# Weight blocks split in one cast and one subtraction of 128x1024 in a hybrid decoder step

## The chip, the cores and the metric

The kernel runs on one core of one Trainium2 chip. The metric is the device time of one execution in microseconds (us). Before the change the median of three runs is 1835.99 us (1828.75 to 1836.97).

## The reference, cut to what matters

The reference is one layer of a decoder over 256 prompt tokens and 8 sample tokens (264 columns in the kernel). Nearly all of its work is a chain of large matrix products:

```python
z = h @ p['w_in'][l]                       # 2048 x 15376
(z_uv, hq, hf, hi, hg, gq, gk, gv, gr, glr, z_gate) = jnp.split(z, offsets, axis=-1)
...                                        # three token mixers: gMLP, HGRN2, GLA
merged = merged + gates[:, :, n_b] * (branches[n_b] @ p['w_branch'][l, n_b])
out = merged @ p['w_out'][l]
x = x + gt1 * rmsnorm(out, p['g_post_mix'][l])
...
y2 = jnp.square(jax.nn.relu(h2 @ p['w_mlp_up'][l])) @ p['w_mlp_down'][l]
x = x + gt2 * rmsnorm(y2, p['g_post_mlp'][l])
```

The two recurrent mixers also read and write a state for each of the 8 samples. All data are fp32.

## The kernel before, in words

**The arithmetic.** A product in fp32 is made of three products in the format fp32r. Each operand is split in a high part (a cast) and a low part (the operand less its high part); `granule` (L649) adds high x high (L659), high x low (L660) and low x high (L661) in PSUM. The activations are split once. The weights are split as they arrive, by the helper `split` (L108): a cast on ScalarE (ACT, L109) and a subtraction on VectorE (DVE, L110, recorded as L106, the line of `sub`). The subtraction reads what the cast wrote.

**Weight blocks.** The class `Stream` (L590) walks through a list of 578 weight blocks, made by `plan` in the order in which TensorE (PE) uses them. A block holds 1024 numbers in each of 128 partitions: four rows of 128x256 in most cases, two rows of 128x512 in the first twenty blocks and in the first MLP product. PE uses a block in 24 matmuls of 264 columns (L659 to L661).

**Stages of a block.** `load` (L596) fetches the block by one DMA, issued from SyncE's queue (SP, L616), into one of four `raw` buffers. Blocks 20 to 71 are fetched in pairs, so that each of two tiles holds a half of two blocks (L598 to L612). `split_half` (L619) splits one half of a block, 128x512, into a tile `whi` and a tile `wlo`; `split` (L626) does so for both halves. The pool `splp` has six buffers for each of the two kinds, which is three blocks. `ahead` (L631) is called before and after the matmuls of a block: it splits two blocks beyond the one in hand and loads up to five beyond it. So, once the matmuls of block i have been issued, block i+3 is split; its two halves go into the buffers that the two halves of block i leave.

**Use.** `granule` takes a block's two pairs of tiles and goes through its rows: rows of the first half first. Where a block has two accumulators (the first twenty blocks and the first MLP product), it goes through all rows for the first accumulator, then through all rows for the second. The accumulators have two buffers (`pmm`), and are emptied by ACT (L825) or DVE (`add`, recorded as L103).

**Order.** PE, SP and GpSimd (POOL) keep the order in which the program is written. In most stages ACT and DVE get theirs from a scheduler that places each instruction when the program is built, and both engines work strictly in that order. Two kinds of other work stand among the splits: evictions of PSUM, and work of the mixers that `background` (L699) deals out between blocks. Among the latter are the sample states (`samples_r`): POOL issues DMAs for a state `st` and for a row of values `vbc`, and ACT (L1103) and DVE (L1105) then update the state. Those two instructions wait for their DMAs, and what is queued behind them on ACT and DVE waits too.

## Time and profile before

| what | value |
| --- | --- |
| median of three runs | 1835.99 us (1828.75 to 1836.97) |
| the profiled execution, its own time | 1832.18 us |
| its span in the trace | 1830.4 us |
| mean TensorE clock granted | 0.997 of full speed |
| busy share: PE, DVE, ACT, POOL | 98%, 65%, 55%, 7% |
| moved by DMA | 442.05 MB, 242 GB/s over the span |

How to read it. Busy time is the time in which at least one instruction of an engine was running; a matmul's end is modelled, so a busy PE need not be at its peak. A row of a group of instructions gives the source line, the engine and operation, what is written and read, the tile's size and the number of instructions; behind the bar stand the total busy time, the mean of one in ns, and the engine's idle time ahead of them with what ended it. A row of the waits reads "who waited <- for whom: us in total, times, longest". In the timeline a row has start, duration, engine, line and operation; in brackets stands the idle time before it and what ended it. "PEld" is the weight load of a matmul.

### The profile page before, as it was taken

What the parts mean: (1) busy time and instruction counts of PE and PEld (TensorE: products, weight loads), DVE (VectorE), ACT (ScalarE), POOL (GpSimd) and SP (SyncE); (2) the same over time, 40 slices, a digit from 0 to 9 for tenths busy, and PEclk for the clock granted to TensorE, in tenths of its full rate; (3) what the DMA queues carried; (4) which work ended last, traced back from release to release, by engine and by line L of the source; (5) the groups of instructions that cost most, each with busy time, mean ns of one, the idle gap of its engine ahead of it and who ended that gap; (6) DMA issues with size and microseconds to landing.
All of it is one profiled execution on the core that took longest, in us unless ns stands there. A gap on an engine that the chain in (4) does not pass through costs nothing.

```text
span 1830.4 us, 42186 instructions
## 1 busy us (share of the span) xinstructions
PE 1788.7 (98%) x17012; PEld 1696.5 (93%) x17012; DVE 1181.8 (65%) x2092; ACT 1000.3 (55%) x1818; POOL 131.3 (7%) x210
## 2 busy tenths in 40 slices
PE   6999999999999999999999999999999999999998
PEld 4889999989988999989999989999999999999997
DVE  4566677787576696566555667555666666666666
ACT  5544364666755765654445666555554545454544
POOL 4221000111111101210000000000000000000000
PEclk9999999999999999999999999999999999999999
DMA  9999697788787788897987964777666666666663
GB/s 326 354 343 304 195 304 231 215 266 276 239 287 233 229 270 278 274 323 250 308 254 265 327 180 146 246 256 227 191 197 194 197 194 196 195 195 196 196 196 106
DMA packets 330179, 442.05 MB, mean 242 GB/s; under 512 B 14946, under 2 KB 276944, under 8 KB 329984
## 3 DMA queue, kind: packets, MB, share of 16 engines
q1 hardware_dynamic: 311728, 380.26, 65.0%
q0 software_dynamic: 17184, 57.85, 9.1%
q8 instruction: 133, 2.18, 0.5%
q10 hardware_dynamic: 1072, 1.25, 0.2%
q14 instruction: 62, 0.51, 0.1%
HBM read 427.60 MB, written 11.70 MB: 240 GB/s over the span
## 4 chain that ended last, share of the span: by engine, by line
PE 88%; DMA 2%; DVE 2%; issue 1%; ACT 1%; POOL 0%; DVEq 0%; ACTq 0%; POOLq 0%
PE mm L659 27%; PE mm L661 26%; PE mm L660 26%; PE ada L376 3%; DMA vbc<-vs_d 1%; PE ada L308 1%; DVE wlo L106 1%; PE sm L851 1%; PE sm L1208 1%; PE sm L679 1%; PE sm L686 1%; DMA raw<-in_w_in_dram 0%; DVE b L106 0%; PE sm L1578 0%; ACT whi L109 0%
## 5 line engine op out<-in xcount | busy, mean ns | idle before, releaser
L659 PE MATMUL mm<-b,whi 128*128 128x264 f32 x4624 | 1292.4, 279 | 12.3 <-issue 5.1
L661 PE MATMUL mm<-b,wlo 128*128 128x264 f32 x4624 | 1279.7, 277 | 5.1 <-DVE wlo L106 4.5
L660 PE MATMUL mm<-b,whi 128*128 128x264 f32 x4624 | 1278.8, 277 | 0.8 <-DVE b L106 0.7
L106 DVE TENSOR_TENSOR wlo<-raw,whi 128x512 fp32r<-128x512 f32 x1136 | 774.4, 689 | 489.1 <-ACT whi L109 475.0
L109 ACT CAST whi<-raw 128x512 fp32r<-128x512 f32 x1136 | 691.8, 616 | 644.5 <-DVE wlo L106 331.7
L659 PEld LDWEIGHTS mm<-b,whi 128*128 128x128 f32 x4624 | 875.8, 189 | 53.0 <-issue 28.0
L661 PEld LDWEIGHTS mm<-b,wlo 128*128 128x128 f32 x4624 | 876.2, 189 | 7.3 <-DVE wlo L106 7.2
L660 PEld LDWEIGHTS mm<-b,whi 128*128 128x128 f32 x4624 | 876.2, 189 | 4.4 <-issue 3.0
L103 DVE TENSOR_TENSOR b<-b,mm 128x528 f32<-128x528 f32 (+1 forms) x137 | 95.7, 699 | 24.5 <-PE mm L661 13.0
L1105 DVE SCALAR_TENSOR_TENSOR st<-vbc,b,st 128x128 f32<-128x128 f32 (+1 forms) x96 | 34.2, 390 | 55.2 <-DMA vbc<-vs_d 50.4
L1103 ACT ACTIVATE st<-st,fs 128x128 f32<-128x128 f32 (+1 forms) x96 | 37.1, 430 | 50.5 <-DMA st<-in_state_hgrn_dram 26.9
L488 POOL DMA_DIRECT2D b<-in_w_ada_dram x64 | 46.2, 724 | 126.0 <-PE ada L308 94.4
L376 PE MATMUL ada<-araw,cT 128*32 128x512 f32 x296 | 39.8, 601 | 0.0
L308 PE MATMUL ada<-b,cT 128*32 128x256 f32 (+1 forms) x640 | 35.1, 356 | 2.8 <-DMA b<-in_w_ada_dram 2.6
L100 DVE TENSOR_TENSOR b<-b,b 128x512 f32<-128x512 f32 (+1 forms) x47 | 33.9, 741 | 1.3 <-ACT b L1221 1.0
L1106 POOL DMA_DIRECT2D out_dram<-st x32 | 23.6, 736 | 130.5 <-DVE st L1105 130.5
L308 PEld LDWEIGHTS ada<-b,cT 128*32 128x32 f32 x640 | 17.8, 113 | 14.9 <-DMA b<-in_w_ada_dram 6.2
L376 PE MATMUL ada<-b,cT 128*32 128x512 f32 x216 | 26.2, 594 | 0.0
L106 DVE TENSOR_TENSOR b<-gt,b 128x528 fp32r<-128x528 f32 x32 | 22.7, 710 | 3.2
L106 DVE TENSOR_TENSOR b<-b 128x1024 f32<-128x1024 f32 (+1 forms) x24 | 24.3, 1017 | 0.0
L1632 ACT ACTIVATE b<-vt 128x528 fp32r<-128x528 f32 x32 | 23.0, 719 | 1.0
L106 DVE TENSOR_TENSOR b<-b,b 128x1056 fp32r<-128x1056 f32 (+3 forms) x21 | 20.8, 991 | 4.0 <-ACT b L109 3.8
(344 smaller groups left out, 854.0 us busy)
## 6 DMA issues: line engine op xcount, KB each, us to landing
raw<-in_w_in_dram SPq DMA_DIRECT2D x231, 512.0 KB, 4.8
raw<-in_w_mlp_up_dram SPq DMA_DIRECT2D x128, 512.0 KB, 3.9
raw<-in_w_mlp_down_dram SPq DMA_DIRECT2D x128, 512.0 KB, 3.7
araw<-in_w_ada_dram SPq DMA_DIRECT2D x74, 512.0 KB, 5.7
b<-in_w_ada_dram SPq DMA_DIRECT2D x54, 512.0 KB, 6.6
b<-in_w_ada_dram POOLq DMA_DIRECT2D x48, 512.0 KB, 8.9
raw<-in_w_branch_dram SPq DMA_DIRECT2D x48, 512.0 KB, 4.5
raw<-in_w_out_dram SPq DMA_DIRECT2D x32, 512.0 KB, 5.3
```

What stands on the lines that cost most here:

```text
L100: V.tensor_tensor(o, a, b, op=ALU.mult)
L103: V.tensor_tensor(o, a, b, op=ALU.add)
L106: V.tensor_tensor(o, a, b, op=ALU.subtract)
L109: S.copy(hi, src)
L308: T.matmul(acc[32 * j:32 * j + 32, 0:n], cT[:, k, :], w[:, n * j:n * j + n], start=k == 0, stop=k == KT - 1)
L376: T.matmul(self.acc[32 * j:32 * j + 32, :], cT[:, k, :], ws[j // 2][:, j % 2 * 512:j % 2 * 512 + 512], start=k == 0, stop=k == KT - 1)
L488: queue.dma_start(w[:, i], w1[k * P:(k + 1) * P, :, self.k0 * P:(self.k0 + self.n) * P])
L659: T.matmul(o, a, xh(k + j), start=first and j == 0, stop=False)
L660: T.matmul(o, a, xl(k + j), start=False, stop=False)
L661: T.matmul(o, b, xh(k + j), start=False, stop=last and j == n - 1)
L1103: S.activation(st[:, i, :], st[:, i, :], AF.Copy, scale=fs[:, h0 + i, b:b + 1])
L1105: V.scalar_tensor_tensor(st[:, i, :], v[:, i, :], k[:, h0 + i, NP + b:NP + b + 1], st[:, i, :], ALU.mult, ALU.add)
```

## The change

Each block that arrives in one tile is split by one cast and one subtraction of 128x1024. The `whi` and `wlo` tiles hold a whole block in every case, and there are three buffers of each kind instead of six of half the size. The first block (fetched by two DMAs) and the paired blocks 20 to 71 are still cast and subtracted in halves, which go into slices of the whole tile. In `granule` the matmuls read slices of one pair of tiles; their order is the same.

```diff
-SPLIT_BUFS = 6
+SPLIT_BUFS = 3
...
-            self.raw[i] = [t[:, 0:n // 2, :], t[:, n // 2:n, :]]
-
-        def split_half(self, i):
+            self.raw[i] = [t[:, 0:n // 2, :], t[:, n // 2:n, :]] if i == 0 else [t]
+
+        def split_next(self, i):
             n, width = self.items[i][2], self.items[i][4]
-            hi = splp.tile([P, n // 2, width], F32R, tag="whi", name=nm("whi"))
-            lo = splp.tile([P, n // 2, width], F32R, tag="wlo", name=nm("wlo"))
-            split(self.raw[i].pop(0), hi, lo)
-            self.parts.setdefault(i, []).append((hi, lo))
+            if i not in self.parts:
+                hi = splp.tile([P, n, width], F32R, tag="whi", name=nm("whi"))
+                lo = splp.tile([P, n, width], F32R, tag="wlo", name=nm("wlo"))
+                self.parts[i], self.done[i] = (hi, lo), 0
+            src = self.raw[i].pop(0)
+            js = slice(self.done[i], self.done[i] + src.shape[1])
+            self.done[i] = js.stop
+            split(src, *(v[:, js, :] for v in self.parts[i]))
...
-        h = n // 2
...
-                    a, b = (p[:, j % h, m * P:(m + 1) * P] for p in parts[j // h])
+                    a, b = (p[:, j, m * P:(m + 1) * P] for p in parts)
```

More of the change, by code (lines that the diff above doesn't have):

```diff
@@ L593, in __init__ @@
         def __init__(self, items):
-            self.items, self.raw, self.parts, self.at = items, {}, {}, 0
+            self.items, self.raw, self.parts, self.done, self.at = items, {}, {}, {}, 0
         def load(self, i):
@@ L616, in load @@
                 nc.sync.dma_start(t[:, a:b, :], w[(k + a) * P:(k + b) * P, c0:c0 + width].rearrange("(k p) c -> p k c", p=P))
-            self.raw[i] = [t[:, 0:n // 2, :], t[:, n // 2:n, :]]
-        def split_half(self, i):
+            self.raw[i] = [t[:, 0:n // 2, :], t[:, n // 2:n, :]] if i == 0 else [t]
+        def split_next(self, i):
             n, width = self.items[i][2], self.items[i][4]
-            hi = splp.tile([P, n // 2, width], F32R, tag="whi", name=nm("whi"))
-            lo = splp.tile([P, n // 2, width], F32R, tag="wlo", name=nm("wlo"))
-            split(self.raw[i].pop(0), hi, lo)
-            self.parts.setdefault(i, []).append((hi, lo))
+            if i not in self.parts:
[6 more added lines that the diff above has]
+            split(src, *(v[:, js, :] for v in self.parts[i]))
         def split(self, i):
             while self.raw[i]:
-                self.split_half(i)
+                self.split_next(i)
             del self.raw[i]
@@ L797, in hybrid_step_kernel @@
     rows = first.rows()
-    stream[0].split_half(0)
+    stream[0].split_next(0)
     next(rows)
@@ L802, in hybrid_step_kernel @@
     run(rows)
-    stream[0].split_half(0)
+    stream[0].split_next(0)
     for k, ps in zip((4, 6), early):
```

## The prediction

> **What bounds the kernel now.** I read the page's totals first, then the forty slices, then who waits for whom.

> ```profile
> span 1830.4 us, 42186 instructions
> PE 1788.7 (98%) x17012; PEld 1696.5 (93%) x17012; DVE 1181.8 (65%) x2092; ACT 1000.3 (55%) x1818; POOL 131.3 (7%) x210
> ...
> L106 DVE TENSOR_TENSOR wlo<-raw,whi 128x512 fp32r<-128x512 f32 x1136 | 774.4, 689 | 489.1 <-ACT whi L109 475.0
> L109 ACT CAST whi<-raw 128x512 fp32r<-128x512 f32 x1136 | 691.8, 616 | 644.5 <-DVE wlo L106 331.7
> ```

> PE is busy for 98% of the span: 41.7 us of idle are all that any change on ACT and DVE can win back. The instructions that the change merges are the largest users of DVE and ACT, but neither engine is full. The slices (PE, PEld, DVE, ACT, POOL busy, then clock, DMA share, GB/s) show three kinds of stage:

> ```profile
> 45.80:91.50 45.70, 42.88 (x494) 38.74 (x496) 25.20 (x43) 23.45 (x42) 12.25 (x17) 1.00 0.96 354
> 549.10:594.90 45.80, 42.94 (x500) 40.66 (x501) 30.51 (x56) 26.54 (x54) 6.64 (x10) 0.96 0.74 233
> 777.90:823.70 45.80, 43.11 (x383) 40.40 (x382) 28.07 (x59) 23.28 (x46) 6.71 (x10) 1.00 0.94 323
> 1372.80:1418.60 45.80, 45.80 (x409) 45.80 (x409) 28.89 (x43) 22.12 (x36) 0.00 (x0) 1.00 0.65 194
> ```

> First a start with DMA at 0.96, then mixers with small holes in PE, then an MLP in which PE never idles. Over the whole span the splits cost PE this:

> ```profile
> PEld mm L659 <- ACT whi L109: 11.7, 15, 1.0
> PEld mm L661 <- DVE wlo L106: 7.2, 11, 2.5
> PE mm L661 <- DVE wlo L106: 4.5, 6, 2.3
> ```

> The last two overlap (a weight load and its matmul), so about 19 us hang on splits.

> **The change: what it removes.** 1156 casts and 1156 subtractions (578 blocks in halves). By the changed kernel's instruction order 525 blocks become whole; the first and the 52 paired ones keep halves. SP's, POOL's and PE's order is the same, and the background work keeps its place among the splits but for half a block to a block, mostly earlier than them. No row is a 128x1024 split of a raw tile; the nearest are a 128x1024 TENSOR_TENSOR in fp32 and ACT's 128x1024:

> ```profile
> L106 DVE TENSOR_TENSOR b<-b 128x1024 f32<-128x1024 f32 x15 | 18.2, 1216 | 0.0
> L1221 ACT ACTIVATE b<-b 128x1024 f32<-128x1024 f32 x3 | 3.2, 1058 | 1.9 <-DVE b L106 1.9
> L1626 ACT ACTIVATE vt<-mm 128x528 f32<-128x528 f32 x32 | 19.4, 605 | 0.8 <-PE mm L661 0.8
> L1632 ACT ACTIVATE b<-vt 128x528 fp32r<-128x528 f32 x32 | 23.0, 719 | 1.0
> L100 DVE TENSOR_TENSOR gt<-vt 128x528 f32<-128x528 f32 x32 | 22.5, 702 | 0.8 <-ACT vt L1626 0.8
> L106 DVE TENSOR_TENSOR b<-gt,b 128x528 fp32r<-128x528 f32 x32 | 22.7, 710 | 3.2
> ```

> I take 1.22 us for the subtraction and 1.06 for the cast. Apart, a pair took 2 x 0.69 and 2 x 0.62, so 0.16 and 0.18 us are saved per block. Where DVE is behind, less: in the timeline below two subtractions took 1.28 us together, so each costs 0.60 of queue, and a 128x1024 took 1.14 until the next began (400.37 to 401.51). There the saving is 0.06 per block. [...]

> **What it adds: a later start and a coarser hand-over.** In the MLP the casts follow PE:

> ```profile
> 1403.09 0.62 ACT L109 CAST whi<-raw 128x512 fp32r<-128x512 f32 x1 [0.73 <-PE mm L660]
> 1408.49 0.62 ACT L109 CAST whi<-raw 128x512 fp32r<-128x512 f32 x1 [0.73 <-PE mm L660]
> ```

> Four casts (two blocks) in 5.40 us: a block lasts 2.70, a half 1.35. A half is split when PE leaves the same half of the block three before; PE needs it two and a half blocks later, 6.75 us, less 0.62 + 0.69 and some 0.03 for the hand-over: 5.41 us to spare. A whole tile comes free only at its block's end, and its low part must be done by the start of the third block after, two blocks later: 5.40 - 1.06 - 1.22 - 0.03 = 3.09 us. In the MLP the work that can stand ahead is at most 0.61 + 0.72 on ACT and 0.70 + 0.71 on DVE; 3.09 still covers both (2.74) if they came one after the other. So **the MLP costs 0**; without this cover, what exceeds 3.09 would be lost once per 10.8 us.

> Loads wait for the raw buffer, which the subtraction releases:

> ```profile
> SPq L616 <- DVE wlo L106: 1054.5, 442, 15.7
> ...
> raw<-in_w_in_dram SPq DMA_DIRECT2D x231, 512.0 KB, 4.8
> ```

> The first is from SP's waits, the second from the DMA issues. The release moves by up to 2.31 - 1.34 = 0.97 us, and with it the load and whatever SP holds behind it. With four raw buffers a load is issued about four blocks, 10.8 us, before its cast is due; 10.8 - 2.3 = 8.5 us still cover a landing of 4.8. I cost it at 0; in stages with DMA at 0.96 the cover may fail, which bounds it by 0.97 us for each of the twenty early blocks, were all of it lost.

> In the mixers the reserve is used. DVE stands still for a DMA of sample values, and the splits behind it wait:

> ```profile
> 397.29 0.88 DVE L1105 SCALAR_TENSOR_TENSOR st<-vbc,b,st 128x128 f32<-128x128 f32 x3 [5.10 <-DMA vbc<-vs_d]
> 519.78 0.61 DVE L1105 SCALAR_TENSOR_TENSOR st<-vbc,b,st 128x128 f32<-128x128 f32 x2 [6.05 <-DMA vbc<-vs_d]
> 597.22 1.14 DVE L1105 SCALAR_TENSOR_TENSOR st<-vbc,b,st 128x128 f32<-128x128 f32 x4 [5.29 <-DMA vbc<-vs_d]
> 678.16 0.88 DVE L1105 SCALAR_TENSOR_TENSOR st<-vbc,b,st 128x256 f32<-128x256 f32 x2 [4.44 <-DMA vbc<-vs_d]
> 715.69 0.49 DVE L1105 SCALAR_TENSOR_TENSOR st<-vbc,b,st 128x256 f32<-128x256 f32 x1 [3.66 <-DMA vbc<-vs_d]
> 781.87 0.88 DVE L1105 SCALAR_TENSOR_TENSOR st<-vbc,b,st 128x256 f32<-128x256 f32 x2 [7.36 <-DMA vbc<-vs_d]
> ```

> Six waits beyond 3.5 us: all exceed 3.09. The first in detail (ACT, DVE, PE):

> ```profile
> 388.47 0.62 ACT L109 CAST whi<-raw 128x512 fp32r<-128x512 f32 x1 [0.94 <-DVE st L1105]
> 396.26 0.99 ACT L1103 ACTIVATE st<-st,fs 128x128 f32<-128x128 f32 x3 [7.17 <-DMA st<-in_state_hgrn_dram]
> 397.15 0.60 ACT L109 CAST whi<-raw 128x512 fp32r<-128x512 f32 x1
> ```
> ```profile
> 390.92 1.28 DVE L106 TENSOR_TENSOR wlo<-raw,whi 128x512 fp32r<-128x512 f32 x2
> ...
> 398.09 0.68 DVE L106 TENSOR_TENSOR wlo<-raw,whi 128x512 fp32r<-128x512 f32 x1
> ...
> 400.37 1.22 DVE L106 TENSOR_TENSOR b<-b 128x1024 f32<-128x1024 f32 x1
> 401.51 0.68 DVE L106 TENSOR_TENSOR wlo<-raw,whi 128x512 fp32r<-128x512 f32 x1
> ```
> ```profile
> 397.81 0.38 PE L659 MATMUL mm<-b,whi 128*128 128x264 f32 x1 [0.26 <-ACT whi L109]
> 398.83 0.38 PE L661 MATMUL mm<-b,wlo 128*128 128x264 f32 x1 [0.53 <-DVE wlo L106]
> ```

> Half a block was cast at 388.47, ahead of ACT's wait of 7.17 us, and PE lived on it until the other half came at 397.15. In the changed order the state updates stand ahead of the whole cast: it starts at 397.15, its subtraction ends near 397.15 + 1.06 + 0.03 + 1.22 = 399.46, and only then PE has the low part with which it began before this wait. What PE used to do meanwhile, **half a block or 1.35 us, is lost once per place**, since the splits behind follow DVE's queue as before. Bounds: 0, if the whole split lands ahead of the wait; 2.32 us, the reserve lost (5.41 - 3.09). I take 1.35, which the place shows: 6 x 1.35 = 8.1 us. Against it, six backlogs of some six blocks save 36 x 0.06 = 2.2.

> One hole more may halve the clock. In the chain of waits this hole of PE stands in the slice with clock 0.96:

> ```profile
> 563.02 2.86 issue
> ```

> 0.04 x 45.8 = 1.8 us were lost there, while the slice from 777.90, with 2.69 us of idle in pieces, kept 1.00. I put one such event in: 1.7 us (0 to six, 10).

> In the first twenty blocks evictions and splits share queues:

> ```profile
> 64.16 1.29 ACT L109 CAST whi<-raw 128x512 fp32r<-128x512 f32 x2 [0.42 <-PE mm L660]
> 65.36 0.60 ACT L825 COPY b<-mm 128x528 f32<-128x528 f32 x1
> ...
> PEld mm L659 <- DVE b L103: 2.8, 3, 1.5
> ```

> The second cast began 0.67 into the 1.29, at the block's end, 64.83; a whole one starts then and delays the eviction from 65.36 to 65.89, 0.5 us, on about three blocks without other PE work between: 1.5 lost. In the next ten blocks both evictions now stand ahead of the split instead of behind its halves, which can save up to the 2.8 us of the last row (waits from 28 to 110 us). I take 0 (-2.8 to +1.5).

> **Sum**: 8.1 - 2.2 + 1.7 + 0 = +7.6 us: 1832.18 becomes 1839.8. The median lay 3.8 above that execution, so 1835.99 + 7.6 = **1843.6 us**, slower by 0.4%. About 0.5% (9.2 us) is what a measurement of this kernel can tell from no change.

> **Rivals.** (a) *Not slower: the lighter queues win.* From the point where DVE's backlog, not the buffer, ends a wait, a whole subtraction finishes earlier than two halves, and evictions come ahead. Price: half of the 19 us of split waits less the 1.35 of two places, -7: 1829. For it: in the mixers DVE works in such backlogs. Against: 0.06 us per block is small, and the waits' ends are landings of DMAs. (b) *The whole reserve is lost at each place, and half clock follows*: 6 x 2.32 + 3 x 1.7 = +19, less 2.2: 1853. For it: six waits exceed 3.09, and a block that waits whole gives one long hole instead of two short ones. [...] (c) *Everything is hidden*, 1836: the scheduler places whole splits ahead of the waits.

> **Chances.** Forecast 0.45, (a) 0.16, (b) 0.25, (c) 0.14. Slower by over 0.5%: (b) and 0.20 of the forecast, whose upper terms pass 9.2: 0.45. Faster: 0.10, of (a). Same: 0.45. Range: from a little above (a), 1830, to above (b) with the early loads, 1859; the forecast's own is 1838 to 1850.

> **What would show it.** Right: subtractions near 1.22 and casts near 1.06; PE at 45.8 of 45.8 in the MLP; PE's waits for `whi` and `wlo` grow by 6 to 12 us near 397, 519, 597, 678, 716 and 782, at the start of blocks. Wrong: holes in the MLP, subtractions far from 1.22, or these waits shrinking.

## The result and the profile after

The changed kernel takes **1847.62 us** (median of four runs, 1847.31 to 1848.14), beside 1836.48 (four runs, 1828.75 to 1838.85) before. The ratio is 1.0072, with a 95% interval of 1.0054 to 1.0089: slower. The two medians differ by 11.1 us. The two profiled executions differ by 15.4 us: 1847.6 against 1832.18, with spans of 1845.8 and 1830.4. The lines below have moved: L659 to L661 are now L662 to L664, and lines further down stand three higher (L851 is L854, L1425 is L1428).

From the page of the changed kernel, the totals and the engines; then the two groups of whole splits, from its groups by shape (count, busy time and mean ns of one, idle time ahead of them and what ended it):

```profile
span 1845.8 us, 40173 instructions
PE 1795.4 (97%) x17012; PEld 1700.6 (92%) x17012; DVE 1124.9 (61%) x1567; ACT 913.7 (50%) x1293; POOL 130.9 (7%) x210
```
```profile
L106 DVE TENSOR_TENSOR wlo<-raw,whi 128x1024 fp32r<-128x1024 f32 x525 | 641.6, 1223 | 437.3 <-ACT whi L109 425.5 <-PE ada L376 7.3 <-PE mm L664 2.2
L109 ACT CAST whi<-raw 128x1024 fp32r<-128x1024 f32 x525 | 546.9, 1044 | 644.3 <-PE mm L663 593.9 <-issue 23.2 <-DMA raw<-in_w_in_dram 8.8
```

The change did what it says. DVE is busy for 56.9 us less (1181.8 to 1124.9), ACT for 86.6 less (1000.3 to 913.7), and 2013 instructions are gone. PE, with the same 17012 matmuls, stands idle for 50.4 us instead of 41.7 and works more often at half clock (0.50 granted, in stretches of 3.41 us): the mean granted clock is 0.994 instead of 0.997. So both engines that were relieved got lighter, and the one that bounds the kernel lost time.

The waits for splits over the whole span, and PE's waits for casts after 1106 us, where before has no such row:

```profile
PEld mm L662 <- ACT whi L109: 15.7, 18, 1.8
...
PEld mm L664 <- DVE wlo L106: 10.7, 11, 2.4
...
PE mm L664 <- DVE wlo L106: 8.6, 10, 2.2
```
```profile
PEld mm L662 <- ACT whi L109: 4.2, 5, 0.8
```

They grew from 11.7 + 7.2 to 15.7 + 10.7, by 7.5 us. Of the last row, 3.4 us lie in the MLP and cost nothing: there a weight load waits, but no matmul does, and the steps are as long as before. Even the 7.5 us aren't the whole loss, nor do these waits stand where most of it is. To find it, I cut both traces at the first matmul of chosen blocks (each block has 24 matmuls of 264 columns, always in the same order) and took the time from cut to cut, in us:

| blocks | stage | before | after | difference |
| --- | --- | --- | --- | --- |
| start to 0 | until the first block | 27.7 | 26.5 | -1.2 |
| 0 to 98 | first twenty blocks, paired blocks | 325.91 | 328.27 | +2.36 |
| 98 to 226 | mixers, with the sample states | 456.99 | 461.73 | +4.74 |
| 226 to 290 | last branch's gates and products | 189.84 | 189.84 | 0 |
| 290 to 322 | w_out, and the step behind it | 102.21 | 110.73 | **+8.52** |
| 322 to 338 | start of the MLP | 52.77 | 53.71 | +0.94 |
| 338 to 577 | MLP | 656.93 | 656.94 | 0 |

The largest piece is the product with `w_out`, for which the prediction had no term. It is also a steady one: this stretch takes 102.21 to 102.23 us in all four profiles of kernels with half tiles, while the mixers vary by some us from execution to execution. PE's waits in that stage, before and after:

```profile
PEld sm L1466 <- DVE a L103: 1.7, 1, 1.7
...
PE sm L1466 <- DVE a L103: 0.8, 1, 0.8
```
```profile
PEld sm L854 <- ACT gt L1431: 5.2, 7, 0.8
PEld sm L1469 <- DVE a L103: 3.8, 1, 3.8
PE sm L1469 <- DVE a L103: 3.6, 1, 3.6
```

None of these is a wait for a split. L854 are transposes on PE: they turn the result of a group of four w_out blocks, which DVE (L1428) and ACT (L1431) have emptied from PSUM, into rows by token. Seven groups, seven waits, 0.8 us at the longest; before, this stage has no row for L851. Behind the last block PE waits for DVE (L103, a sum of squares): 3.8 instead of 1.7.

One of the seven groups in the timeline, first of the changed kernel (ACT, DVE, weight load of PE), then of before:

```profile
1066.28 1.04 ACT L109 CAST whi<-raw 128x1024 fp32r<-128x1024 f32 x1 [1.66 <-PE mm L663]
...
1069.01 0.47 ACT L1431 ACTIVATE gt<-mm,G 128x256 f32<-128x256 f32 x1 [1.18 <-DVE gt L1428]
...
1067.36 1.23 DVE L106 TENSOR_TENSOR wlo<-raw,whi 128x1024 fp32r<-128x1024 f32 x1 [1.48 <-ACT whi L109]
...
1068.50 0.48 DVE L1428 TENSOR_SCALAR gt<-mm,G 128x256 f32<-128x256 f32 x1
...
1069.54 0.42 PEld L854 LDWEIGHTS sm<-cst,gt 128*128 128x128 f32 x4 [0.68 <-ACT gt L1431]
```
```profile
1033.79 0.62 ACT L109 CAST whi<-raw 128x512 fp32r<-128x512 f32 x1 [0.61 <-PE mm L660]
...
1035.67 0.47 ACT L1428 ACTIVATE gt<-mm,G 128x256 f32<-128x256 f32 x1
...
1034.44 0.69 DVE L106 TENSOR_TENSOR wlo<-raw,whi 128x512 fp32r<-128x512 f32 x1 [0.53 <-ACT whi L109]
1035.05 0.48 DVE L1425 TENSOR_SCALAR gt<-mm,G 128x256 f32<-128x256 f32 x1
...
1036.32 0.45 PEld L851 LDWEIGHTS sm<-cst,gt 128*128 128x128 f32 x4
```

On DVE the eviction is queued behind a split, and ACT's eviction follows DVE's. Before, only the second half of that split was still to do when PE left the block: from the start of its cast (1033.79) the split took 1.34 us, the evictions were done after 2.35 (1036.14), and PE came to the transposes after 2.53, without a wait. After, the whole split starts when PE leaves the block, and its two instructions run one after the other: the split takes 2.31 us from 1066.28, the evictions are done after 3.20 (1069.48), and the transposes start after 3.26. That is 0.73 us later. By the cuts the block that holds the transposes takes 3.76 us instead of 3.06, 0.70 more.

In three of the seven groups it takes 4.18 to 4.20. There PE's order itself has changed: small matmuls of another product (`ada`, L376) have come forward from behind w_out; where they stand is settled when the program is built. One such group, and the step behind the last block, in the changed kernel:

```profile
1044.22 1.06 PE L376 MATMUL ada<-b,cT 128*32 128x512 f32 x8
...
1045.22 0.66 PE L854 MATMUL sm<-cst,gt 128*128 128x128 f32 x4
...
1102.11 1.04 ACT L109 CAST whi<-raw 128x1024 fp32r<-128x1024 f32 x1 [1.66 <-PE mm L663]
...
1105.76 0.61 PE L1469 MATMUL sm<-cst,a 128*128 128x1 f32 x4 [3.57 <-DVE a L103]
```

and the step behind the last block before:

```profile
1089.99 0.62 ACT L109 CAST whi<-raw 128x512 fp32r<-128x512 f32 x1 [0.73 <-PE mm L660]
...
1089.99 1.92 PE L376 MATMUL ada<-b,cT 128*32 128x512 f32 x16
...
1092.67 0.61 PE L1466 MATMUL sm<-cst,a 128*128 128x1 f32 x4 [0.75 <-DVE a L103]
```

Sixteen matmuls of L376 that used to fill the wait behind the last block now stand in three groups (2, 8 and 6 of them), where they take longer than the wait that they fill. The last wait lies bare: 3.57 us instead of 0.75. From cast to L1469 pass 3.65 us instead of 2.68, 0.97 more, which is what the split takes longer (2.31 less 1.34); half clock follows (0.50 granted from 1106.60 to 1110.01), and the step is 2.28 longer (17.72 against 15.44). The stage is then accounted for: four groups at 0.70, three at 1.13 (4.19 less 3.06) and 2.28 for the last step make 8.5 us.

The 0.94 us at the start of the MLP look like the same thing: there DVE's scaling (L1561), on which PE's transposes (L1581) depend, stands behind a split. The step of block 324 takes 5.70 us instead of 5.05, and 5.06 in the kernel below that splits whole tiles in halves.

### The profile page after: what moved, and what is told of

It is laid out like the page before. It is cut to its first block, busy times and chain, and to the rows that moved or that the text cites. A ratio compares the mean times of both kernels' runs of the same rounds, so it can differ in the third digit from the quotient of the medians.

```text
span 1845.8 us, 40173 instructions
## 1 busy us (share of the span) xinstructions
PE 1795.4 (97%) x17012; PEld 1700.6 (92%) x17012; DVE 1124.9 (61%) x1567; ACT 913.7 (50%) x1293; POOL 130.9 (7%) x210
## 4 chain that ended last, share of the span: by engine, by line
PE 86%; DVE 5%; DMA 4%; issue 2%; ACT 2%; POOL 0%; SPq 0%; DVEq 0%; ACTq 0%; POOLq 0%
PE mm L662 26%; PE mm L664 26%; PE mm L663 26%; PE ada L376 3%; DVE wlo L106 2%; PE ada L308 1%; DMA vbc<-vs_d 1%; ACT whi L109 1%; DMA raw<-in_w_in_dram 1%; PE sm L854 1%; PE sm L1211 1%; DMA st<-in_state_gla_dram 1%; PE sm L689 1%; PE sm L682 0%; DVE b L100 0%
## 5 line engine op out<-in xcount | busy, mean ns | idle before, releaser
L662 PE MATMUL mm<-b,whi 128*128 128x264 f32 x4624 | 1293.2, 280 | 8.2 <-ACT whi L109 2.6
L664 PE MATMUL mm<-b,wlo 128*128 128x264 f32 x4624 | 1281.2, 277 | 8.6 <-DVE wlo L106 8.6
L106 DVE TENSOR_TENSOR wlo<-raw,whi 128x1024 fp32r<-128x1024 f32 (+1 forms) x611 | 697.1, 1147 | 441.5 <-ACT whi L109 429.5
L109 ACT CAST whi<-raw 128x1024 fp32r<-128x1024 f32 (+1 forms) x611 | 596.0, 984 | 714.1 <-PE mm L663 661.1
L662 PEld LDWEIGHTS mm<-b,whi 128*128 128x128 f32 x4624 | 877.2, 190 | 51.5 <-issue 24.3
L664 PEld LDWEIGHTS mm<-b,wlo 128*128 128x128 f32 x4624 | 877.3, 190 | 12.5 <-DVE wlo L106 10.7
L103 DVE TENSOR_TENSOR b<-b,mm 128x528 f32<-128x528 f32 (+1 forms) x137 | 95.5, 699 | 100.7 <-PE mm L664 100.7
L1108 DVE SCALAR_TENSOR_TENSOR st<-vbc,b,st 128x128 f32<-128x128 f32 (+1 forms) x96 | 32.9, 389 | 66.4 <-DMA vbc<-vs_d 58.9
L376 PE MATMUL ada<-araw,cT 128*32 128x512 f32 x296 | 39.8, 601 | 0.0
L100 DVE TENSOR_TENSOR b<-b,b 128x512 f32<-128x512 f32 (+1 forms) x47 | 33.4, 741 | 4.5 <-ACT b L1171 1.7
L376 PE MATMUL ada<-b,cT 128*32 128x512 f32 x216 | 28.3, 611 | 0.0
L106 DVE TENSOR_TENSOR b<-gt,b 128x528 fp32r<-128x528 f32 x32 | 22.7, 709 | 3.6 <-DVE gt L100 0.5
L106 DVE TENSOR_TENSOR b<-b 128x1024 f32<-128x1024 f32 (+1 forms) x24 | 24.3, 1015 | 0.0
L100 DVE TENSOR_TENSOR gt<-vt 128x528 f32<-128x528 f32 x32 | 22.5, 702 | 0.0
## 6 DMA issues: line engine op xcount, KB each, us to landing
raw<-in_w_in_dram SPq DMA_DIRECT2D x231, 512.0 KB, 4.7
raw<-in_w_mlp_up_dram SPq DMA_DIRECT2D x128, 512.0 KB, 3.9
raw<-in_w_mlp_down_dram SPq DMA_DIRECT2D x128, 512.0 KB, 3.7
araw<-in_w_ada_dram SPq DMA_DIRECT2D x74, 512.0 KB, 6.0
b<-in_w_ada_dram SPq DMA_DIRECT2D x54, 512.0 KB, 6.3
b<-in_w_ada_dram POOLq DMA_DIRECT2D x48, 512.0 KB, 8.0
raw<-in_w_branch_dram SPq DMA_DIRECT2D x48, 512.0 KB, 4.6
raw<-in_w_out_dram SPq DMA_DIRECT2D x32, 512.0 KB, 4.4
```

What stands on the lines that cost most here:

```text
L100: V.tensor_tensor(o, a, b, op=ALU.mult)
L103: V.tensor_tensor(o, a, b, op=ALU.add)
L106: V.tensor_tensor(o, a, b, op=ALU.subtract)
L109: S.copy(hi, src)
L376: T.matmul(self.acc[32 * j:32 * j + 32, :], cT[:, k, :], ws[j // 2][:, j % 2 * 512:j % 2 * 512 + 512], start=k == 0, stop=k == KT - 1)
L662: T.matmul(o, a, xh(k + j), start=first and j == 0, stop=False)
```

## The experiments

Three theories stood against each other. The letters in the quoted texts belong to those texts; in words the theories are:

- **The mixers** (the prediction): the whole tile is handed over later, and at each long wait of DVE for a DMA PE loses half a block.
- **The eviction behind the split**: the loss lies where an eviction on which PE depends stands behind a split, since a whole split takes longer from its start to its end.
- **The tile or the instruction**: three whole tiles change when a buffer comes free; whole instructions change how long a split takes. Either could carry the loss in both places.

### The transposes one block later, in both kernels

```diff
-            later.append((now[0], lambda m=m, g=g: block_rows(m, g)))
+            later.append((now[0] + 1, lambda m=m, g=g: block_rows(m, g)))
```

This moves the transposes of a w_out group (L854) one block further along PE's order, so that the eviction has 2.7 us more. It was made in the changed kernel and in the one before.

> The changed kernel, with the transposes of each output column group (block_rows) dealt out one block later. Theory A (in the stage of w_out the whole split stands ahead of the eviction on DVE, and the transposes come one block after the group's end, before the eviction is done): the seven PE waits of 0.7 to 1.1 us between 1015 and 1095 vanish, PE's weight loads there no longer wait for ACT gt; the time falls by 6 us against the changed kernel, to about 1841.5. Rival B (the loss there is the larger instructions' occupation of DVE or ACT): the time stays at 1847 to 1848.

> The kernel before, with the same transposes one block later: the control for rows_later. Theory A: PE does not wait there in the kernel before, so nothing is won: 1836, within 2 us. Rival B' (the later transposes are better by themselves): 2 us or more below the kernel before.

Measured: the changed kernel with the edit takes 1839.61 us (four runs, 1838.86 to 1845.45), ratio 1.0047 (1.0028 to 1.0066) to before; the kernel before with the edit 1835.19, ratio 1.0008 (0.9994 to 1.0022). The stretch of blocks 290 to 322 fell from 110.73 to 104.29 us, while in the kernel before it stayed (102.23). The wait of L854 has no row any more, and the matmuls of L376 stand behind w_out again. That return is part of the gain: in the change a step with L376 took 4.19 us and one without 3.76, so it is worth 3 x 0.43 = 1.3 us, and no run moves L376 alone. What is left of the stage's loss, 2.1 us, lies in its last step (17.52 us against 15.44), with half clock behind the wait below (eight matmuls of L376 took 1.91 us from 1105.10, where sixteen took 1.92 from 1100.20):

```profile
PEld sm L1469 <- DVE a L103: 2.6, 1, 2.6
PE sm L1469 <- DVE a L103: 1.7, 1, 1.7
```

So the eviction behind the split, with what it does to L376, carries some 6.4 us, in a place where the kernel before has nothing to win. The ratios' intervals still overlap that of the change (1.0054 to 1.0089), so here the stage, not the total, is what shows it.

### Sample values fetched earlier, in both kernels

```diff
-FETCHED = 3
+FETCHED = 5
```

> The changed kernel, with each sample state update placed two blocks later behind its DMAs (FETCHED 5 instead of 3). Theory A (what the mixers lost is reserve used up while ACT and DVE wait for the DMAs of states and values): DVE's wait for vbc falls from 59 us to under 20, PE's waits for whi and wlo near 390, 520, 787 and 804 shrink, and 4 to 7 us are won: about 1842. Rival B (the mixers lost by the order and size of the instructions, not by those waits): within 2 us of 1847.6.

> The kernel before with FETCHED 5: the control for fetched5. Theory A: the kernel before had less to lose at the same waits, so it wins less than the changed kernel, 1 to 4 us: about 1834. Rival B: it wins as much as the changed kernel does, or both nothing.

Both missed. The changed kernel went to 1870.76 us (1.0215, 1.0196 to 1.0233), the one before to 1850.87 (1.0098, 1.0079 to 1.0116). DVE's waits for `vbc` did not shrink: 67.7 us in 23 and 54.0 in 20, against 58.9 and 50.4 in 19 each. Instead the sample work finished late, and PE stood idle ahead of block 178 for 15.5 and 11.7 us. The waits were moved, not taken away, so this says nothing on the mixers. One thing can be read from it: the w_out stretch differs by as much as ever, 111.63 against 102.22.

### Whole tiles, half instructions

```diff
-            self.raw[i] = [t[:, 0:n // 2, :], t[:, n // 2:n, :]] if i == 0 else [t]
+            self.raw[i] = [t[:, 0:n // 2, :], t[:, n // 2:n, :]]
```

The changed kernel with its three whole tiles, but with two casts and two subtractions of 128x512 for every block.

> The changed kernel's three whole tiles, but every block cast and subtracted in two halves, each into its slice. Theory A (the tile decides: no cast may start before the last matmul of the block three before, and that is late for the mixers and for the eviction behind the splits): as slow as the changed kernel or little better, 1843 to 1848. Rival B (the size of the instructions decides, since an eviction waits behind 1.05 + 1.22 us instead of 0.62 + 0.69): near the kernel before, 1834 to 1838.

Measured: 1838.39 us (ten runs, 1834.88 to 1843.57), ratio 1.0017 (1.0004 to 1.003). This interval lies clear of the change's. So the coarser hand-over of tiles costs about 0.17%, some 3 us, and **the size of the instructions the other 8 of 11**. Its w_out stretch took 105.24 us, its mixers 457.27. The same place of w_out in its timeline, and its row of the waits:

```profile
1049.55 1.14 ACT L109 CAST whi<-raw 128x512 fp32r<-128x512 f32 x2 [1.56 <-PE mm L663]
...
1051.92 0.47 ACT L1431 ACTIVATE gt<-mm,G 128x256 f32<-128x256 f32 x1 [0.73 <-DVE gt L1428]
...
1050.20 1.29 DVE L106 TENSOR_TENSOR wlo<-raw,whi 128x512 fp32r<-128x512 f32 x2 [1.41 <-ACT whi L109]
1051.41 0.48 DVE L1428 TENSOR_SCALAR gt<-mm,G 128x256 f32<-128x256 f32 x1
...
1052.45 0.42 PEld L854 LDWEIGHTS sm<-cst,gt 128*128 128x128 f32 x4 [0.32 <-ACT gt L1431]
```
```profile
PEld sm L854 <- ACT gt L1431: 2.2, 7, 0.3
```

Both casts start at the block's end, as the whole one does, since the tile is the same. But the first subtraction starts at 1050.20, while the second cast still runs. The split is done 1.94 us after its start (1051.49 less 1049.55), the whole one after 2.31, and the one half that was left before after 1.34. Evictions and transposes follow in this order, and so do the steps, in us:

| | before | half instructions in whole tiles | the change |
| --- | --- | --- | --- |
| split at the group's end, start to end | 1.34 | 1.94 | 2.31 |
| transposes start after | 2.53 | 2.90 | 3.26 |
| step of the block with the transposes | 3.06 | 3.40 | 3.76 |
| step behind the last block | 15.44 | 16.04 | 17.72 |

Its matmuls of L376 all stand behind w_out, as before.

### Without the DMAs of states and values, in both kernels

```diff
-            nc.gpsimd.dma_start(st, G.s_in(b, h, nh))
...
-            v = tmp([P, 4, P], "vbc", VB_BUFS)
-            r0 = 4 * nj * b + h * nj
-            nc.gpsimd.dma_start(v, vs_d[G.i, r0:r0 + 4, :].partition_broadcast(P))
-            vals.append((v.rearrange("p (h j) v -> p h (j v)", h=nh), now[0]))
+            vals.append((cst[:, 0:256], now[0]))
...
-                S.activation(st[:, i, :], st[:, i, :], AF.Copy, scale=fs[:, h0 + i, b:b + 1])
+                S.activation(st[:, i, :], v[:, 0:dv], AF.Copy, scale=fs[:, h0 + i, b:b + 1])
...
-                V.scalar_tensor_tensor(st[:, i, :], v[:, i, :], k[:, h0 + i, NP + b:NP + b + 1], st[:, i, :], ALU.mult, ALU.add)
+                V.scalar_tensor_tensor(st[:, i, :], v[:, 0:dv], k[:, h0 + i, NP + b:NP + b + 1], st[:, i, :], ALU.mult, ALU.add)
```

The update instructions stay and read a constant, so that nothing waits for `st` or `vbc`; the sample states and their outputs are left out of the computation.

> The kernel before without the DMAs of sample states and values: both update instructions read a constant tile instead, so that ACT and DVE never wait for those DMAs (the sample states and outputs are left out of the computation). Theory A: PE's waits for whi and wlo between 354 and 811 us nearly go, some 3 to 6 us are won: 1828 to 1833. Its use is as the control of after_nodma.

> The changed kernel without the same DMAs (the sample states and outputs are left out). Theory A (in the mixers the change loses where ACT or DVE wait for a DMA longer than the smaller reserve): the loss against the control between 354 and 811 us, 5.5 us in the profiles of the two kernels, falls below 1.5; the loss in the stage of w_out (6 us) and behind it (3 us) stays, so it is 7 to 10 us above before_nodma. Rival B (the mixers lose by the size or order of the instructions): the 5.5 us stay.

Measured: 1818.93 us for the kernel before (ratio 0.9913, 0.9896 to 0.9929) and 1830.01 for the changed one (0.998, 0.9967 to 0.9992). The DMAs were worth more than expected, 16 us, but in both kernels alike: without them the changed kernel is **still 11.1 us behind**. If each of the six waits had cost it half a block, the difference would have fallen to a few us. The mixers' own loss was expected to fall below 1.5 us, and that failed too: in the profiled execution (the slowest of ten, 1835.38) they took 446.52 us against 442.50; 3.6 of these 4.0 lie between blocks 146 and 160, at one hole of 1.88 us with half clock behind it (the other 1.7 is what one stretch of 3.41 us at 0.50 costs). The w_out stretch took 111.62 against 102.21. What the DMAs do not carry, w_out does.

### Four whole tiles

```diff
-RAW_BUFS = 4
+RAW_BUFS = 3
...
-SPLIT_BUFS = 3
-NBLK = 28
+SPLIT_BUFS = 4
+NBLK = 27
```

A fourth tile would give back the reserve that the coarser hand-over takes. One `raw` buffer and one background tile were given up for it.

> The changed kernel with four whole tiles of each kind; to make room, one raw buffer and one block buffer fewer (3 and 27). Theory A (the reserve decides): a split may start a block earlier, the reserve grows from 3.1 to 5.8 us; PE's waits for whi and wlo in the mixers fall to those of the kernel before, and the cast and subtraction of w_out's stage can be done before the eviction is due: 1836 to 1840. Rival B (instruction size): 1845 or more. Rival C: the missing raw buffer costs more than the fourth tile brings, seen as ACT's casts waiting for DMAs: above 1850.

Measured: 1872.41 us (1.02, 1.0177 to 1.0224). The casts now wait for the loads:

```profile
ACT whi L109 <- DMA raw<-in_w_in_dram: 110.2, 66, 4.2
```

In the changed kernel this row reads 9.2 us in 6 waits. The missing raw buffer hides what the fourth tile gave over the whole span; a fourth tile by itself was not tried. In w_out, where no cast waits for a load, the steps with transposes took 3.76 to 4.20 us as in the changed kernel, and L854 waited 5.2 us in 7: there a fourth tile did not bring the cast forward.

### One of the two merged alone

Whole tiles in both; `h` is half the rows of the block. First one cast of 128x1024 and two subtractions of 128x512, then two casts and one subtraction:

```diff
-            split(src, *(v[:, js, :] for v in self.parts[i]))
...
+            S.copy(hi, src)
...
+            for s in (slice(0, h), slice(h, 2 * h)):
+                sub(lo[:, s, :], src[:, s, :], hi[:, s, :].bitcast(F32))
```
```diff
-            split(src, *(v[:, js, :] for v in self.parts[i]))
...
+            for s in (slice(0, h), slice(h, 2 * h)):
+                S.copy(hi[:, s, :], src[:, s, :])
+            sub(lo, src, hi.bitcast(F32))
```

> The changed kernel with one whole cast and two half subtractions. Theory C (the loss is the overlap: with halves the second cast runs beside the first subtraction, so a block is split in 1.14 + 0.7 = 1.9 us; whole, 1.05 + 1.22 = 2.3 us in series): 1.05 + 1.29 = 2.3 us, as slow as the changed kernel, 1845 to 1849, PE waits of 0.7 to 1.1 us in each group of w_out. Rival D (the loss is DVE's long instruction ahead of the evictions): near the three whole tiles split in halves, 1837 to 1840.

> The changed kernel with two half casts and one whole subtraction. Theory C: 1.14 + 1.22 = 2.4 us in series, as slow as the changed kernel or a little slower, 1846 to 1851. Rival D: as slow as the changed kernel as well, while its counterpart is fast. Rival E (the loss is ACT's long cast ahead of ACT's evictions): 1837 to 1840.

Measured: 1845.9 us (six runs, ratio 1.0059, 1.0044 to 1.0075) with the whole cast, and 1858.36 (four runs, 1.0125, 1.0112 to 1.0139) with the whole subtraction. Neither is near the 1838.39 of both in halves. From the timelines, in the MLP where nothing else stands between, first with the whole cast, then with the whole subtraction:

```profile
1503.24 1.05 ACT L632 CAST whi<-raw 128x1024 fp32r<-128x1024 f32 x1 [1.65 <-PE mm L670]
...
1504.31 1.29 DVE L106 TENSOR_TENSOR wlo<-raw,whi 128x512 fp32r<-128x512 f32 x2 [1.40 <-ACT whi L632]
```
```profile
1502.61 1.14 ACT L634 CAST whi<-raw 128x512 fp32r<-128x512 f32 x2 [1.56 <-PE mm L670]
...
1503.78 1.23 DVE L106 TENSOR_TENSOR wlo<-raw,whi 128x1024 fp32r<-128x1024 f32 x1 [1.47 <-ACT whi L634]
```

Either way the first subtraction starts when the last cast ends, and the split takes 2.36 and 2.40 us, as long as the whole one. It took both in halves to overlap them (1.94 us). The transposes of w_out wait as in the changed kernel (here L854 is L861), 4.8 us in the first and 5.6 in the second:

```profile
PEld sm L861 <- ACT gt L1438: 4.8, 6, 0.8
```
```profile
PEld sm L861 <- ACT gt L1438: 5.6, 7, 0.8
```

With the whole cast, the step of a block with transposes is 3.83 to 3.87 us where no L376 stands (3.76 in the change), and both kernels have the sixteen matmuls of L376 in w_out as the change has. The w_out stretches took 112.14 and 111.22 us. In the mixers the two part: 455.00 us with the whole cast (before: 456.99), 473.08 with the whole subtraction, 16.1 more than before, of which 13.4 lie between blocks 200 and 226, where PE waits up to 4.8 us for `wlo`. That the second would be slower than the change itself was not expected, and why its mixers are so much longer is open.

### Halves in w_out alone

```diff
-            self.raw[i] = [t[:, 0:n // 2, :], t[:, n // 2:n, :]] if i == 0 else [t]
+            self.raw[i] = [t[:, 0:n // 2, :], t[:, n // 2:n, :]] if i == 0 or 290 <= i < 322 else [t]
```

> The changed kernel with halves only in the 32 blocks of w_out. Theory C: the seven PE waits there shrink from 0.7 to 1.1 us to 0.3, 3 to 5 us are won, and nothing elsewhere: 1842 to 1845. Rival: the gain of the halves came from the mixers, then 1847.

Measured: 1846.56 us (six runs, 1842.17 to 1847.24), ratio 1.0055 (1.0041 to 1.0068). The stage did what was expected: 105.58 us, 5.15 less than in the changed kernel. The total did not: in its profiled execution the mixers took 463.97 us, 2.2 longer than in the changed kernel, and the time until block 20 was 1.9 longer. The edit touches none of that code, and the instructions up to block 226 stand in the same order in all three traces. So single executions of the same mixer code differ by some us (461.73 in the change, 464.45 with the transposes later, 463.97 here), and a total of few runs doesn't resolve five.

### Both: whole tiles, half instructions, transposes later

The edits of "whole tiles, half instructions" and "one block later" together.

> Three whole tiles split in halves, with the transposes of block_rows one block later. Theory C: the remaining seven waits of 0.3 us go too, 2 to 3 us below the same kernel without it, level with the kernel before: 1834 to 1837. Rival (whole tiles lose in the mixers as well): it stays at 1838 or more.

Measured: 1837.34 us (twelve runs, 1833.33 to 1839.91), ratio 1.0008 (0.9998 to 1.0019): level with before. The w_out stretch is back at 102.81; the mixers of the profiled execution took 460.37. With both causes out, nothing measurable of the loss is left in the total, and nothing is won either. No version beat the kernel before.

## Why the prediction was right or wrong

The sign, the size within a few us (1843.6 against 1847.62) and the range held. The sum held less well than its result, and that the total came near is in part luck: the mixers, priced at 7.6 us, gave 4.74 in the profiles, and 8.52 came from a stage priced at nothing.

**Right: the durations.** 1.22 and 1.06 were taken for a whole subtraction and cast; 1223 and 1044 ns were measured. Each merged pair is cheaper (1223 ns against 2 x 689 on DVE, 1044 against 2 x 616 on ACT), and the kernel still got slower: these rows count an engine's busy time, and here the latency of a chain over two engines decided (2.31 us whole, 1.94 in halves).

**Right: the MLP costs nothing.** 656.94 against 656.93 us. The reserve of 3.09 us, worked out from 1.06 and 1.22 in series, was enough. So the same series was in the prediction's hands; it was only asked whether PE's next split would be late, not what else stood behind it.

**Wrong: nothing stands behind the splits outside the first twenty blocks and the mixers.** This is the step that failed. The prediction had the background work keep its place, "mostly earlier than them", asked for evictions behind splits in the first twenty blocks only, and let w_out go without a term. There the eviction stands behind a split that ends 0.97 us later, with some 0.1 us to spare (transposes after 2.53, evictions done after 2.35 and 0.06 for the hand-over). Also wrong, in the same stage: "SP's, POOL's and PE's order is the same". PE's is not, for the sixteen matmuls of L376. The program writes them in fours and they run in groups of 2, 8 and 6, so there PE does not keep the written order, other than the description of the kernel says. Both together made +8.5 us of the profiled difference, more than half. Moving the transposes took 6.4 of it away, overlapping the halves 5.5, both together 7.9.

**Partly wrong: half a block is lost once per place in the mixers.** Six places at 1.35 less 2.2 for shorter queues, with a clock event of 1.7, gave 7.6; the mixers became 4.74 longer. The 1.7 was an estimate beside the 1.8 that its row gave; in the clock records of before and after a stretch lasts 3.41 us at a granted 0.50, which makes 1.7. PE's waits for splits near the six places (397, 519, 597, 678, 716, 782) grew from 0.8, 1.1, 0, 0, 0 and 2.7 us to 1.4, 2.9, 0.4, 0.5, 0 and 4.2, by 4.8 in place of 8.1. So the waits grew, 3.9 of it at the first, second and last place, at little over half the price. At 519, before and after:

```profile
521.67 0.38 PE L661 MATMUL mm<-b,wlo 128*128 128x264 f32 x1 [0.68 <-DVE wlo L106]
```
```profile
524.04 0.59 PE L664 MATMUL mm<-b,wlo 128*128 128x264 f32 x1 [2.19 <-DVE wlo L106]
```

The first place, worked out in detail, went like this in the changed kernel (ACT, DVE, PE):

```profile
394.56 1.28 ACT L1106 ACTIVATE st<-st,fs 128x128 f32<-128x128 f32 x4 [6.39 <-DMA st<-in_state_hgrn_dram]
395.75 1.98 ACT L109 CAST whi<-raw 128x1024 fp32r<-128x1024 f32 x2
...
396.47 1.14 DVE L1108 SCALAR_TENSOR_TENSOR st<-vbc,b,st 128x128 f32<-128x128 f32 x4 [4.51 <-DMA vbc<-vs_d]
397.52 1.22 DVE L106 TENSOR_TENSOR wlo<-raw,whi 128x1024 fp32r<-128x1024 f32 x1
...
398.80 0.38 PE L664 MATMUL mm<-b,wlo 128*128 128x264 f32 x1 [0.61 <-DVE wlo L106]
```

The order is the one predicted: states first, then the whole cast and its subtraction. But the state landed 1.7 us earlier than in the execution before (394.56 against 396.26), the low part was there at 398.74 instead of the 399.46 worked out, and PE waited 0.61 us (1.4 with two smaller waits at 386.70 and 402.29), beside 0.26 + 0.53 before. Where a wait ends with a DMA, one execution's landing is no constant to which a delay can be added.

These waits alone aren't the loss. With half instructions in the same whole tiles they came to 8.3 us at the six places, with the whole cast alone to 9.0, and the mixers of these two took 457.27 and 455.00 us, level with before (456.99). That they are level is in part luck with the clock: in these two no half clock fell into the mixers, where before has two stretches of 3.4 us and the change three, while PE stood idle there for 13.1 and 11.2 us, against 10.6 before and 13.8 in the change. Of the change's 4.74 us, then, 3.25 are idle time of PE and 1.5 are slower matmuls.

The other profiled executions with the same order of instructions put a scale to this: 464.45 and 463.97 us with the order of the change, 459.02 with that of before, 460.37 with half instructions in whole tiles. So the mixers seem to lose some 5 us with whole instructions and about 1 with whole tiles alone; with two or three executions of each it stays an estimate. How much of it hangs on DMAs stays open as well: without them the 11.1 us stayed, and 4.0 of it in the mixers of the one execution profiled.

**Right for the mixers: one clock event more.** Over the whole span there were three more: one near 110 us (below) and one in the last step of w_out. In the slice of 0.96, the execution before, the hole of 2.86 us was followed by 3.41 us at a granted 0.50 (566.67 to 570.08).

**Right: the first twenty blocks cost about 0** (78.77 against 78.85 us), **and the loads cost nothing there**. The +2.36 us of blocks 0 to 98 lies behind them: 1.67 is a half-clock stretch near 110 us, and 0.77 stands between blocks 80 and 98, where the kernels with half tiles all took 60.25 us and those with whole tiles 60.9 to 61.6.

**The rivals.** Rival (b), the whole reserve lost, asked for six places at 2.32 us and three half-clock events, and isn't what happened (the waits grew by 4.8 us, one event came); rival (a): the queues got lighter and the kernel no faster, only blocks 178 to 200 took less (-1.18 us); rival (c), everything hidden, holds for the MLP.

## What to carry to other kernels

Here, where a cast on ACT feeds a subtraction on DVE, two halves of each overlapped (1.94 us from first start to last end), and one whole pair ran in series (2.31), though each engine was busy for less. Before such a merge, list every eviction or other instruction with a deadline of PE that stands behind the pair in either queue, in each stage, and set the later end against the time to spare there; here the deadline with 0.1 us to spare was the one that paid. A slack of 3 us for the next tile tells nothing of what else is queued.

## What the runs showed of the hardware that was not expected

**Half clock came after windows in which PE was idle for about half the time.** Windows of before and after around a hole of 1.47 us in PE at block 20, which all these kernels but the one with three raw buffers have (columns: length, busy time of PE, PEld, DVE, ACT, POOL, then the granted clock, DMA share, GB/s); the last row is at 520 us after the change:

```profile
105.00:115.00 10.00, 7.73 (x60) 7.10 (x61) 7.52 (x16) 4.26 (x7) 0.72 (x1) 1.00 1.04 405
```
```profile
105.00:115.00 10.00, 7.54 (x45) 6.96 (x46) 5.69 (x12) 3.05 (x6) 0.72 (x1) 0.83 0.97 373
520.00:530.00 10.00, 7.12 (x36) 6.73 (x36) 9.51 (x14) 6.08 (x12) 0.00 (x0) 0.66 0.53 185
```

Half clock (0.50) for a time t lowers the mean of 10 us by t/20: 0.83 is 3.4 us, 0.66 is 6.8, two such stretches. PE lost 1.67 us to the first one, between blocks 20 and 80 (188.48 against 186.81), and the kernel before without its sample DMAs lost the same. It came in nine of ten profiled executions of kernels with whole tiles and in two of four with half tiles; a tie to the change is neither shown nor excluded.

**A second cast or subtraction of 128x512 in a row cost less than the first.** Two casts took 1.14 us, with 0.62 for one alone; two subtractions 1.29, with 0.69 for one. A whole cast (1.05) therefore saved ACT only 0.09 us of queue, and a whole subtraction (1.22) only 0.07 on DVE.
